# One decoder layer on one core: the modulation matvec in wider steps, wider gate columns, and a shorter last sum

## The chip, the cores and the metric

The program runs on one core of a Trainium2 chip. The metric is the device time of one execution in microseconds (us), inputs and weights in device memory, all arithmetic in f32. Engines are named as in the profile: PE (TensorE), DVE (VectorE), ACT (ScalarE), POOL (GpSimd), SP (SyncE, which here only issues DMAs).

## What is computed

One layer of a hybrid decoder, on 1024 prompt tokens and 8 single-token samples (1032 columns), model width 2048. Cut to what matters here:

```python
mod = silu(c) @ w_ada + b_ada                  # 2048 -> 3 x 2048, for 9 rows of c
shift, scale, gate = split(mod, 3)
h = rmsnorm(x, norm_g) * (1 + scale) + shift
z = h @ w_in                                   # 2048 -> 8208
y_a = b_a * conv3(c_a * h_a) * silu(g_a)       # group A, 1024 channels
o   = gated_delta_rule(conv4+silu of q|k|v, beta, decay)   # group B, 8 heads of 128, chunked
y = concat(y_a, rmsnorm(o) * silu(g_b)) @ w_out
x = x + gate * y;  return rmsnorm(x, final_g)  # and the conv and delta-rule states
```

## The kernel before

Everything is kept feature by token: a "feature tile" is 128 features on the partitions, 16 of them make up the 2048. The tokens go through in two halves of 512, the samples with the second. Each f32 product of a projection is three matmuls on rounded parts (`hh` x `whi`, `hl` x `whi`, `hh` x `wlo`); `raw` is a weight tile as loaded, `whi` and `wlo` its two parts, made by ACT and by POOL or DVE. A small planner (`_Order`) runs while the program is written. It has cost numbers for each instruction and transfer, and where code says `fill`, `pump`, `yield` or `spawn` it decides what is written next; on the chip each engine then runs its list in that order. So changed cost numbers (`_transfer`, the `cost=` of matmuls) change the order everywhere behind them.

Three places matter.

**First stage** (0 to about 169 us). The 16 tiles of x are loaded (`x`), squared and summed (`norm`, `rstd_of`). Then `w_ada` comes in 64 loads of 512 KB (`units`, `load_ada`, tiles `wat`, nine buffers), the first 2 x 2048 of its columns: shift (`s_` 0) and scale (`s_` 1). PE multiplies them with `sc` (silu of c, 9 of 32 columns used): the stationary operand has only 32 columns, so four matmuls of different k sit side by side on four strips of 32 columns of the array (`tile_position=(0, 32 * j)`), and their sums land in four bands of 32 partitions of one PSUM tile. ACT copies that to `ev`, and matmuls with the constant `selada` (10 columns) add the four bands and turn features to the partitions. DVE adds the biases into `sh` and `s1`, and `make_h` builds `hh` and `hl`. Step by step over the feature tiles (`steps`: 1, 1, then six steps of 2, then 1, 1) the tile's products with seven column groups of `w_in` are accumulated (`first_products`, PSUM tiles `pss`); `fill` puts such products between the matvec's matmuls where it expects PE to wait for a load. The stage ends with the logits' matmuls (`wlt`).

**Gates** (240 to 520 us). The third 2048 columns of `w_ada` are needed only by the output. `gate_chunks` takes them beside the first half's work: 64 loads `gw` of 256 KB (four k tiles by 128 columns), a block of 8 matmuls of 128 columns for each two of them, every `GATES` us, again on four strips; per 512 columns a copy `evg` and four `selada` matmuls.

**End.** The second half's last output product goes to `res`. `settle` squares it (ACT) and adds the square to `acc` (DVE). `final` waits for all 16, `rstd_of` sums `acc` over features with a matmul by ones, POOL takes the power, PE spreads the result, ACT copies it to `rf`. DVE (11 tiles, from PSUM) and POOL (5 tiles, from `rf`) scale the 16 tiles of `res`, and SP writes them out in 8 DMAs of two tiles.

Of the kernel before, what the change touches and what calls it, by code (L numbers as in the profile page):

```python
# [40 lines left out]
for _n, _w in [("ident", 128), ("selada", 10), ("sell", 16), ("tri", 128), ("m4", 4), ("eye", 128), ("hmask", 8),  # L41
               ("krow", 1), ("shup", 128), ("shdn", 128), ("perm", 128)]:
    CK[_n] = (_off, _w)
    _off += _w
# [5 lines left out]
def _consts():  # L50
# [4 lines left out]
    for r in range(P):  # L55
# [9 lines left out]
        if r % 32 < 9:  # L65
            c["selada"][r, r % 32] = 1
# [230 lines left out]
def _transfer(src, dst):  # L297

    n = _size(dst) * dst.shape[0]
    if src.tensor.name == "in_w_in" and int(src.offset) % 8208 // P % 8 in SLOW:  # L300
        return n * 4 / 66e3
    run = n
    for ap in (src, dst):
        r = 1
        for s, k in reversed([(int(s), int(k)) for s, k in ap.ap]):
            if s != r:
                break
            r *= k
        run = min(run, r)
    return n * 4 / (210e3 if run <= 128 else 290e3) if run >= 128 else n / run * 0.005  # L310
# [74 lines left out]
def _trunk(ctx, tc, nc, xT, w_in, w_ada, w_out, pack, consts, vecs, csq, ssm, yT, cap, cqp, ssp, cas, cqs, sss):  # L385
# [76 lines left out]
    def rstd_of(acc, n, out, now=False):  # L462
# [5 lines left out]
        yield [acc[:, :n], 2 * MARGIN]  # L468
# [3 lines left out]
        for c in range(nf):  # L472
            mm(ps[:, c:c + 1], acc[:, c * P:(c + 1) * P], ones[:, 0:1], start=True, stop=True)
        if w:
            mm(ps[:w, nf:nf + 1], acc[:, nf * P:n], ones[:, 0:1], start=True, stop=True)
            V.tensor_scalar(sm[:w, nf:nf + 1], ps[:w, nf:nf + 1], 1.0 / D, EPS, ALU.mult, ALU.add)
        V.tensor_scalar(sm[:, :nf], ps[:, :nf], 1.0 / D, EPS, ALU.mult, ALU.add)
# [7 lines left out]
        if w:  # L485
            p3 = p2[:, nf * P:n] if n <= 512 else ch_tile()[:, :w]
            mm(p3, sm[:w, nf:nf + 1].to_broadcast([w, P]), ident[:w, :w], is_transpose=True)
        S.activation(out[:, :nf * P], p2[:, :nf * P], AF.Copy)
        if w:
            S.activation(out[:, nf * P:n], p3, AF.Copy)  # L490
        if now:
            return p2
# [15 lines left out]
    def settle(t, a, b, first, fg=None):  # L508
# [12 lines left out]
        if not first:  # L521
# [862 lines left out]
    def norm():  # L1384

        ps = ch_tile()
        for k in range(NK):
# [5 lines left out]
            if k in PSQ:  # L1393
                mm(ps[:], ident, sqt[:, :HT], start=(k == PSQ[0]), stop=(k == PSQ[-1]))
                continue
            V.tensor_tensor(acc[:, :HT], acc[:, :HT], sqt[:, :HT], ALU.add)
            if k == NK - 3:
                V.tensor_tensor(acc[:, :HT], acc[:, :HT], ps[:], ALU.add)
        normed.append((yield from rstd_of(acc, HT, rstd, True)))
    PSQ, normed = (2, 5, 8, 11), []  # L1400

    hs = []
    with ExitStack() as pools:
# [18 lines left out]
        def first_products(step):  # L1422

            f, nf = steps[step]
# [30 lines left out]
        pump()  # L1455
        for step, (f, nf) in enumerate(steps):
            ps = tp_tile()
            while done < len(units) and units[done][0] == f:
                _, _, s_, k0, nk = units[done]
                wt = wats[done]  # L1460
                if k0 == 0 and s_ == 0:
                    fill(od.ready(ps[:], True))
                fill(od.ready(wt[:], False), 3)
                for k in range(k0, k0 + nk):
                    j = k % 4
                    mm(ps[32 * j:32 * j + 32, s_ * nf * P:(s_ + 1) * nf * P], sc[:, k, :],
                       wt[:, (k - k0) * nf * P:(k - k0 + 1) * nf * P], cost=0.0725 * nf,
                       start=(k < 4), stop=(k >= 12), tile_position=(0, 32 * j))
                wats[done] = None
                done += 1  # L1470
                load_ada()
                k = done - 16
                if 0 <= k < 48 and k % 3 == 0:
                    k //= 3
                    if k == 0:
                        lr_ = fx_tile("lr")
                        lr = lr_[:, :256].rearrange("p (k n) -> p k n", n=16)
                    SY.dma_start(lr[:, k, :], w_in[k * P:(k + 1) * P, 8192:8208])
                if done < len(units) and units[done][0] == f:
                    pump()  # L1480
            if step == 0:
                while not normed:
                    od.advance()
                ws.ahead(1)
            ts = []
            for k in range(f, f + nf):
                ts.append(scaled(xs0[k], HT, rstd if step else normed[0]))
                xs0[k] = None
            ev = tp.tile([P, WH], F32, tag="zr", name="ev")
            S.activation(ev[:, :2 * nf * P], ps[:, :2 * nf * P], AF.Copy)  # L1490
            pump()
            fill(od.ready(ev[:], False))
            for i in range(2 * nf):
                mm(ps[:, i * 10:i * 10 + 10], ev[:, i * P:(i + 1) * P], ck("selada"), start=True, stop=True)
            for i in range(nf):
                k = f + i
                o = (nf + i) * 10
                V.tensor_scalar(sh[:, k, :], ps[:, i * 10:i * 10 + 9], pkv("bada", k, 1), None, ALU.add)
                V.tensor_scalar(s1[:, k, :], ps[:, o:o + 9], b1[:, k:k + 1], pkv("ng", k, 1), ALU.add, ALU.mult)
            od.first(ps_g, "tp", ps)  # L1500
            if step == 0:
                pss = [mm_tile(), mm_tile(), mm_tile(), tp_tile(), ch_tile(), o_tile(), ch_tile()]
            if f % 4 == 0:
                hs += h_quad()
            for k, t in zip(range(f, f + nf), ts):
                make_h(k, t, HT, *hs[k])
            queue.append((f + nf - 1, first_products(step)))
# [22 lines left out]
    GATES = 7.0  # L1530

    def gate_chunks():
# [3 lines left out]
        def load(i):  # L1536
            f, kq = divmod(i, 4)
            wt = fx_tile("gw")
            src = w_ada[kq * 512:(kq + 1) * 512, 2 * D + f * P:2 * D + (f + 1) * P]
            SY.dma_start(wt[:, :512].rearrange("p (k n) -> p k n", n=P), src.rearrange("(k p) n -> p k n", p=P))  # L1540
            tiles.append(wt)
        for i in range(4):
            load(i)
        for f in range(NK):
            if f % 4 == 0:
                ps = mm_tile()
                od.pin(ps)
            for i in (4 * f, 4 * f + 2):
                yield GATES
                yield [tiles[i][:], tiles[i + 1][:], LAND]  # L1550
                for k in range(i % 4 * 4, i % 4 * 4 + 8):
                    j = k % 4
                    mm(ps[32 * j:32 * j + 32, f % 4 * P:(f % 4 + 1) * P], sc[:, k, :],
                       tiles[f * 4 + k // 4][:, j * P:(j + 1) * P], cost=0.096 if k % 8 else 0.18,
                       start=(k < 4), stop=(k >= 12), tile_position=(0, 32 * j))
                tiles[i] = tiles[i + 1] = None
                for j in (4, 5):
                    if i + j < 4 * NK:
                        load(i + j)
            if f % 4 < 3:  # L1560
                continue
# [302 lines left out]
```

## Time and profile before

| what | us |
|---|---|
| median of three runs (lowest, highest) | 2184.36 (2179.47, 2185.21) |
| the profiled execution: its time | 2179.28 |
| its span, first to last instruction | 2177.5 |
| PE busy in the span | 2116.6 (97%) |
| DVE, ACT, POOL busy | 1243.7, 829.3, 826.4 |

A row of the stretches view gives start and end of a stretch, its length, then busy time (and instructions) of PE, PE's weight loads, DVE, ACT and POOL, the granted PE clock (1 is full), the mean busy share of the 16 DMA engines, and GB/s. A row of the timeline gives start, duration, engine, line, operation, output<-inputs, shapes and count; in brackets stands how long the engine had been idle before it, and what released it. Each f32 matmul that is neither rounded nor a transpose appears as two records, so `x8` of the matvec is four matmuls. PE's instructions overlap, so start-to-start times say what one costs. L323 and L372 are lines of helpers that issue every instruction; a group is known by its tile names.

### The profile page before, as it was taken

What the parts mean: (1) busy time and instruction counts of PE and PEld (TensorE: products, weight loads), DVE (VectorE), ACT (ScalarE), POOL (GpSimd) and SP (SyncE); (2) the same over time, 40 slices, a digit from 0 to 9 for tenths busy, and PEclk for the clock granted to TensorE, in tenths of its full rate; (3) what the DMA queues carried; (4) which work ended last, traced back from release to release, by engine and by line L of the source; (5) the groups of instructions that cost most, each with busy time, mean ns of one, the idle gap of its engine ahead of it and who ended that gap; (6) DMA issues with size and microseconds to landing.
All of it is one profiled execution on the core that took longest, in us unless ns stands there. A gap on an engine that the chain in (4) does not pass through costs nothing. (4 is left out here: it accounts for less than half of the span.)

```text
span 2177.5 us, 40451 instructions
## 1 busy us (share of the span) xinstructions
PE 2116.6 (97%) x15045; PEld 1858.7 (85%) x15045; DVE 1243.7 (57%) x3653; ACT 829.3 (38%) x1887; POOL 826.4 (38%) x801
## 2 busy tenths in 40 slices
PE   6999999999999999999999999999999999999996
PEld 3568777777778888878889999999999999999996
DVE  3436766745967636278124747657486486345544
ACT  3224333333443432353233334343343433344553
POOL 1223333433433434332434333344433343444453
PEclk8999999999999999999999999999999999999999
DMA  9984766887544456865434565557673445878777
GB/s 298 327 237 82 157 141 152 136 134 128 135 110 92 90 99 86 76 176 177 148 108 110 122 122 106 118 101 107 105 96 82 96 100 96 90 91 231 213 215 214
DMA packets 507557, 299.65 MB, mean 138 GB/s; under 512 B 37600, under 2 KB 486880, under 8 KB 507360
## 3 DMA queue, kind: packets, MB, share of 16 engines
q1 hardware_dynamic: 484656, 285.31, 61.9%
q10 hardware_dynamic: 22704, 11.77, 2.2%
q8 instruction: 118, 1.93, 0.4%
q14 instruction: 79, 0.65, 0.1%
HBM read 277.06 MB, written 19.94 MB: 136 GB/s over the span
## 5 line engine op out<-in xcount | busy, mean ns | idle before, releaser
L323 POOL TENSOR_TENSOR wlo<-raw,whi 128x512 fp32r<-128x512 f32 x529 | 709.1, 1343 | 1242.3 <-ACT whi L323 1067.9
L372 PE MATMUL mm<-hh,whi 128*128 128x264 f32 (+1 forms) x3008 | 972.5, 323 | 6.3 <-DVE y L323 2.1
L372 PE MATMUL mm<-hl,whi 128*128 128x264 f32 (+1 forms) x3008 | 971.0, 323 | 1.9 <-DVE hl L323 1.9
L372 PE MATMUL mm<-hh,wlo 128*128 128x264 f32 (+1 forms) x3008 | 971.3, 323 | 0.3 <-POOL wlo L323 0.3
L323 ACT ACTIVATE whi<-raw 128x512 fp32r<-128x512 f32 x672 | 418.8, 628 | 622.7 <-PE mm L372 377.6
L372 PEld LDWEIGHTS mm<-hh,whi 128*128 128x128 f32 x3008 | 568.5, 189 | 54.4 <-issue 8.5
L372 PEld LDWEIGHTS mm<-hl,whi 128*128 128x128 f32 x3008 | 568.8, 189 | 43.5 <-DVE hl L323 3.6
L372 PEld LDWEIGHTS mm<-hh,wlo 128*128 128x128 f32 x3008 | 568.6, 189 | 40.4 <-issue 1.0
L372 PE MATMUL mm<-yhi,wlo 128*128 128x512 f32 (+2 forms) x768 | 248.0, 323 | 6.7 <-DVE wlo L323 4.8
L372 PE MATMUL mm<-yhi,whi 128*128 128x512 f32 (+2 forms) x768 | 246.4, 321 | 0.3 <-ACT whi L323 0.2
L372 PE MATMUL mm<-ylo,whi 128*128 128x512 f32 (+2 forms) x768 | 246.2, 321 | 0.0
L323 DVE TENSOR_TENSOR ob<-tb,xb 128x62 f32<-128x62 f32 (+30 forms) x992 | 195.7, 237 | 3.9 <-DMA tb<-ub 3.9
L323 DVE TENSOR_TENSOR xb<-xb,ob 128x62 f32<-128x62 f32 (+30 forms) x992 | 193.6, 235 | 0.0
L323 DVE TENSOR_TENSOR wlo<-raw,whi 128x512 fp32r<-128x512 f32 x143 | 107.1, 754 | 98.5 <-ACT whi L323 76.4
L372 PEld LDWEIGHTS mm<-yhi,wlo 128*128 128x128 f32 x768 | 144.5, 188 | 21.7 <-DVE wlo L323 6.9
L372 PEld LDWEIGHTS mm<-ylo,whi 128*128 128x128 f32 x768 | 144.7, 188 | 12.6 <-issue 1.0
L372 PEld LDWEIGHTS mm<-yhi,whi 128*128 128x128 f32 x768 | 144.6, 188 | 12.1 <-ACT whi L323 0.9
L323 DVE SCALAR_TENSOR_TENSOR kq<-zr,pk,kq 128x512 f32<-128x512 f32 x96 | 103.5, 1078 | 3.4
L323 DVE SCALAR_TENSOR_TENSOR res<-mm,ga,xr 128x512 f32<-128x512 f32 (+2 forms) x48 | 27.3, 569 | 110.7 <-PE mm L372 101.1
L323 DVE TENSOR_TENSOR acc<-acc,sqt 128x512 f32<-128x512 f32 (+3 forms) x71 | 54.7, 773 | 26.1 <-ACT sqt L323 25.1
L323 DVE SCALAR_TENSOR_TENSOR rt<-cht,gt_neg,v 128x128 f32<-128x128 f32 x56 | 19.5, 348 | 72.0 <-PE cht L372 72.0
L323 ACT ACTIVATE u<-cht,sm 128x128 f32<-128x128 f32 x64 | 23.5, 367 | 89.1 <-DVE u L323 76.0
(403 smaller groups left out, 1979.8 us busy)
## 6 DMA issues: line engine op xcount, KB each, us to landing
raw<-in_w_in SPq DMA_DIRECT2D x488, 256.0 KB, 5.0
raw<-in_w_out SPq DMA_DIRECT2D x160, 256.0 KB, 3.4
wat<-in_w_ada SPq DMA_DIRECT2D x64, 512.0 KB, 7.3
gw<-in_w_ada SPq DMA_DIRECT2D x64, 256.0 KB, 6.2
tb<-ub ACTq DMA_DIRECT2D x16, 512.0 KB, 6.5
raw<-in_w_in SPq DMA_DIRECT2D x48, 128.0 KB, 6.0
sl<-in_ssm SPq DMA_DIRECT2D x12, 512.0 KB, 6.3
x1s<-in_xT SPq DMA_DIRECT2D x16, 260.0 KB, 5.2
```

The costliest lines, as they stand in the source:

```text
L323: r = f(*args, **kw)
L372: r = self.pe.matmul(out, lhsT, rhs, **kw)
```

## The change

The first stage keeps its data flow, but goes in five steps of 2, 2, 4, 4 and 4 feature tiles. A `wat` load holds 4 k by 256 columns in the first two steps (rows of 1 KB in memory) and 2 k by 512 columns in the others (rows of 2 KB; before 512 B or 1 KB). A step of four takes shift and scale apart, each a full PSUM tile of 512 columns. PE takes two loads per block. The `selada` matmuls become transposes by `ident`, and DVE adds the four bands with a `tensor_reduce`. Of the sum of squares, the tiles 6, 9, 12 and 15 go through PE instead of 2, 5, 8 and 11.

The gates' loads become one k by 512 columns (2 KB rows), in 16 blocks of four matmuls of 512 columns, one per strip, every 14 us instead of every 7; the `selada` matmuls there become transposes, a reduce and one addition.

At the end the last square is kept out of `acc`: a second pair of matmuls by ones sums it, and DVE adds the two sums. The first of the scaled tiles is put ahead of ACT's copy to `rf`, and every second output DMA is issued by ACT. Some planner numbers change too.

```diff
-    return n * 4 / (210e3 if run <= 128 else 290e3) if run >= 128 else n / run * 0.005
+    return n * 4 / (210e3 if run <= 128 else 290e3 if run < 512 else 340e3) if run >= 128 else n / run * 0.005
...
-    def rstd_of(acc, n, out, now=False):
+    def rstd_of(acc, n, out, now=False, more=None):
...
-        yield [acc[:, :n], 2 * MARGIN]
+        yield [acc[:, :n], 2 * MARGIN if now else LAND]
...
+        if more is not None:
+            V.tensor_scalar(sm[:, :nf], ps[:, :nf], 1.0 / D, EPS, ALU.mult, ALU.add)
+            while not more:
+                yield 0.1
+            yield [more[0]]
+            ps = ch_tile()
+            for c in range(nf):
+                mm(ps[:, c:c + 1], more[0][:, c * P:(c + 1) * P], ones[:, 0:1], start=True, stop=True)
+            V.scalar_tensor_tensor(sm[:, :nf], ps[:, :nf], 1.0 / D, sm[:, :nf], ALU.mult, ALU.add)
...
-        if not first:
+        if keep is not None:
+            keep.append(sqt[:, a:b])
+        elif not first:
             yield [sqt[:, a:b]]
             V.tensor_tensor(acc[:, a:b], acc[:, a:b], sqt[:, a:b], ALU.add)
...
-        steps = [(0, 1), (1, 1)] + [(f, 2) for f in range(2, NK - 2, 2)] + [(NK - 2, 1), (NK - 1, 1)]
-        units = [(f, nf, s_, kq * 4 * nk, 4 * nk) for f, nf in steps for nk in (3 - nf,) for s_ in range(2)
-                 for kq in range(4 // nk)]
+        steps = ((0, 2), (2, 2), (4, 4), (8, 4), (12, 4))
+        units = [(f, nf, s_, k, 8 // nf) for f, nf in steps for s_ in range(2) for k in range(0, NK, 8 // nf)]
...
-            while most and od.now < t and queue and od.ready(hs[queue[0][0]][1], False) <= od.now:
+            while most and od.now < t and queue and max(od.ready(hs[queue[0][0]][1], False), od.now) + 0.35 < t:
...
+        def matvec(f, nf, which, then=None):
...
+                few = units[done:done + (1 if nf == 1 else 2)]
...
+                        mm(ps[32 * j:32 * j + 32, c:c + n], sc[:, k, :], wats[done][:, (k - k0) * n:(k - k0 + 1) * n],
+                           cost=0.0575 * nf + (0.18 if k == few[0][3] else 0.0), start=(k < 4), stop=(k >= 12),
+                           tile_position=(0, 32 * j))
...
+        def spread(ps, f, nf, which):
...
+            S.activation(ev[:, :n * P], ps[:, :n * P], AF.Copy)
...
+            for i in range(n):
+                mm(ps[:, i * P:(i + 1) * P], ev[:, i * P:(i + 1) * P], ident, is_transpose=True)
...
+            V.tensor_reduce(sm[:, :n, :], mk(ps[:], 0, [[P, n], [1, 9], [32, 4]]), AX.X, ALU.add)
...
-    GATES = 7.0
+    GATES = 14.0
...
+                k, f = i % NK * P, 2 * D + i // NK * 512
+                SY.dma_start(tiles[i][:, :512], w_ada[k:k + P, f:f + 512])
...
+            yield [t[:] for t in tiles[i:i + 4]] + [LAND]
+            for j in range(4):
+                mm(ps[32 * j:32 * j + 32, :], sc[:, k + j, :], tiles[i + j][:, :512], cost=0.23 if j else 0.41,
+                   start=(k == 0), stop=(k == 12), tile_position=(0, 32 * j))
...
-                    while settled.get((a, b), 0) < NK:
+                    while settled.get((a, b), 0) < NK - bi:
...
-                            V.tensor_tensor(t, t, r_[:, :b - a], ALU.mult)
+                            V.tensor_tensor(t, t, (r_ if bi else rf)[:, :b - a], ALU.mult)
+                        if bi and m == 0:
+                            S.activation(rf[:, :b - a], r_[:, :b - a], AF.Copy)
...
-                            SY.dma_start(dst, res[m // 4][:, m % 4 + 1 - n:m % 4 + 1, a:b])
+                            (S if bi and m % 4 == 1 else SY).dma_start(dst, res[m // 4][:, m % 4 + 1 - n:m % 4 + 1, a:b])
```

How the order moves is seen on PE at the start: the list up to the first product of the projection (`mm<-hh,whi`), before. `tpt<-wat,sc` are the matvec's matmuls, 16 of 128 columns being two loads; `cht<-ones,acc` and `cht<-cs,rsm` belong to the norm.

```order
L372 MATMUL cht<-sqt,cs 128x512 x4
L372 MATMUL tpt<-wat,sc 32x128 x16
L372 MATMUL cht<-ones,acc 128x1 x4
L372 MATMUL cht<-cs,rsm 128x128 x4
L372 MATMUL tpt<-cs,ev 128x10 x2
L372 MATMUL tpt<-wat,sc 32x128 x8
L372 MATMUL mm<-hh,whi 128x512
```

(A second row of 16 matvec matmuls, left out here, stands between the two rows of the norm.) Five loads are thus taken before the first product. The same list now:

```order
L370 MATMUL cht<-sqt,cs 128x512 x4
L370 MATMUL tpt<-wat,sc 32x256 x8
L370 MATMUL cht<-ones,acc 128x1 x4
L370 MATMUL tpt<-wat,sc 32x256 x16
L370 MATMUL cht<-cs,rsm 128x128 x4
L370 MATMUL tpt<-wat,sc 32x256 x8
L370 MATMUL tpt<-cs,ev 128x128 x4
L370 MATMUL tpt<-wat,sc 32x256 x16
L370 MATMUL mm<-hh,whi 128x512
```

Eight loads now stand ahead of the first transposes, and four more (the last row of 16) ahead of the first product: twelve in all.

The second place is the end of the program on DVE (its last instructions), before; `rsm` is the mean square, `res` the output tiles:

```order
L323 TENSOR_TENSOR res<-res,xr 128x8
L323 TENSOR_TENSOR acc<-acc,sqt 128x256
L323 TENSOR_SCALAR rsm<-cht 128x2
L323 TENSOR_TENSOR res<-res,cht 128x256 x11
L1849 UNCONDITIONAL_BRANCH
```

And now, with what each row waits for:

```order
L321 TENSOR_TENSOR res<-res,xr 128x8 [waits DVE_49]
L321 TENSOR_SCALAR rsm<-cht 128x2 [waits PE_49]
L321 SCALAR_TENSOR_TENSOR rsm<-cht,rsm 128x2 [waits DVE_49,PE_49]
L321 TENSOR_TENSOR res<-res,cht 128x256 [waits PE_49]
L321 TENSOR_TENSOR res<-res,cht 128x256 [waits Activation_49]
```

The addition to `acc` is gone from the end of the list and a second small operation on `rsm` is in. The first scaled tile no longer waits for ACT, but the second does, and ACT's copy in turn (not shown) waits for the first.

The third place is PE's list in the gates: the last block of a column group, with the `evg` matmuls behind it and instructions of the projection and of a head's chain between; before:

```order
L372 MATMUL mm<-gw,sc 32x128 x8
L372 MATMUL mm<-hh,whi 128x512
L372 MATMUL cht<-rt,Y 128x128
L372 MATMUL mm<-hl,whi 128x512
L372 MATMUL mm<-hh,wlo 128x512
L372 MATMUL cht<-cs,evg 128x10 x4
```

There are 32 such `gw` rows in the list, one for each two loads. Now:

```order
L370 MATMUL mm<-gw,sc 32x512 x4
L370 MATMUL mm<-hh,whi 128x512
L370 MATMUL cht<-v,Y 128x128
L370 MATMUL mm<-hl,whi 128x512
L370 MATMUL mm<-hh,wlo 128x512
L370 MATMUL cht<-cs,evg 128x128 x4
```

There are 16 such rows now, one for each four loads; the `evg` rows stay four in number.

More of the change, by code (lines that the diff above doesn't have):

```diff
@@ new lines, in _trunk, with first_norm @@
+        few0 = len([u for u in units if u[0] == 0])
+        def first_norm(done):
+            while len(normed) < (4 if done > few0 // 2 else 2):
+                od.advance()
+        lr = None
+        for step, (f, nf) in enumerate(steps):
+            if nf == 4:
+                for _ in spread(matvec(f, nf, (0,)), f, nf, (0,)):
+                    pass
+            which = (1,) if nf == 4 else (0, 1)
+            ps = matvec(f, nf, which, None if step else first_norm)
+            spreading = spread(ps, f, nf, which)
+            next(spreading)
+            ts = [scaled(xs0[k], HT, rstd if step else normed[3]) for k in range(f, f + min(nf, 2))]
@@ L1481, in _trunk @@
             if step == 0:
-                while not normed:
-                    od.advance()
+                S.activation(rstd[:, :HT], normed[3][:], AF.Copy)
                 ws.ahead(1)
[L1485 to L1491, printed above, removed]
@@ L1500, in _trunk @@
-            od.first(ps_g, "tp", ps)
+            for _ in spreading:
+                pass
             if step == 0:
                 pss = [mm_tile(), mm_tile(), mm_tile(), tp_tile(), ch_tile(), o_tile(), ch_tile()]
[L1503 to L1507, printed above, removed]
+            for k in range(f, f + nf):
+                if k % 4 == 0:
+                    hs += h_quad()
+                make_h(k, ts[k - f] if k - f < 2 else scaled(xs0[k], HT, rstd), HT, *hs[k])
+                xs0[k] = None
+                if nf == 1 or k % 2:
+                    w = min(nf, 2)
+                    queue.append((k, first_products(k + 1 - w, w)))
```

159 lines of the change are left out of this document (82 added, 77 removed).

## The prediction

> **What bounds the kernel now.** I read the page first (PE 97% busy), then the stretches view cut at the first product, the end of the first stage and the ends of the gates, then the timelines of PE and of the end.
>
> ```profile
> 32.40:56.50 24.10, 19.26 (x166) 11.63 (x164) 5.78 (x12) 2.20 (x4) 1.01 (x1) 0.92 1.09 328
> 56.50:169.30 112.80, 110.07 (x797) 70.04 (x798) 41.16 (x70) 30.84 (x50) 30.25 (x27) 0.99 0.92 269
> 169.30:240.00 70.70, 70.70 (x331) 57.88 (x330) 47.35 (x83) 35.59 (x87) 24.78 (x28) 1.00 0.50 103
> 240.00:520.00 280.00, 278.14 (x1840) 216.25 (x1839) 184.68 (x679) 98.08 (x239) 105.32 (x103) 0.99 0.79 144
> 520.00:2163.80 1643.80, 1622.54 (x11812) 1494.09 (x11810) 946.70 (x2771) 645.76 (x1480) 655.62 (x624) 1.00 0.60 123
> 2163.80:2177.50 13.70, 1.04 (x6) 0.71 (x6) 4.94 (x16) 1.31 (x3) 4.15 (x6) 0.69 0.46 153
> ```
>
> Until 56 us PE waits and the DMA engines are full (share 1.09). From 56.5 to 2163.8 PE waits 2.7 + 0 + 1.9 + 21.3 us in all, so what is taken off PE's list there comes off the end almost whole. In the last 13.7 us PE has nothing left and a chain over ACT, DVE, POOL and DMA decides.
>
> **The loads.** The rate depends on the length of a row in memory. The four stretches hold, in turn, only `x` loads (2 KB rows), `wat` loads of 128 columns (512 B), of 256 columns (1 KB), and output DMAs (1 KB):
>
> ```profile
> 6.00:14.00 8.00, 4.84 (x6) 1.30 (x6) 4.33 (x7) 7.18 (x13) 0.00 (x0) 1.00 1.05 402
> 18.00:22.00 4.00, 2.90 (x36) 2.06 (x36) 0.96 (x2) 0.00 (x0) 0.00 (x0) 0.57 1.16 290
> 50.00:59.00 9.00, 5.48 (x57) 2.55 (x56) 2.77 (x7) 3.50 (x6) 0.79 (x1) 0.84 1.10 352
> 2170.00:2175.00 5.00, 0.00 (x0) 0.00 (x0) 1.65 (x5) 0.00 (x0) 1.42 (x3) 0.50 1.04 343
> ```
>
> 524,288 B take 1.81 us at 290 GB/s, 1.49 at 352, 1.30 at 402. PE's waits for loads confirm the first two (20.19 - 18.47, 53.05 - 51.54):
>
> ```profile
> 18.47 1.08 PE L372 MATMUL tpt<-wat,sc 128*32 128x128 f32 x16 [2.81 <-DMA wat<-in_w_ada]
> 20.19 1.08 PE L372 MATMUL tpt<-wat,sc 128*32 128x128 f32 x16 [0.63 <-DMA wat<-in_w_ada]
> ...
> 31.41 1.08 PE L372 MATMUL tpt<-wat,sc 128*32 128x128 f32 x16 [2.93 <-DMA wat<-in_w_ada]
> 32.42 0.80 PE L372 MATMUL mm<-hh,whi 128*128 128x512 f32 x1
> ...
> 51.54 0.64 PE L372 MATMUL tpt<-wat,sc 128*32 128x256 f32 x8 [0.92 <-DMA wat<-in_w_ada]
> 53.05 0.64 PE L372 MATMUL tpt<-wat,sc 128*32 128x256 f32 x8 [0.87 <-DMA wat<-in_w_ada]
> ```
>
> No row shows `w_ada` in 2 KB rows; between 352 (no better than 1 KB) and 402 I take 402, since `x` goes the same way, from memory to the chip on the same queue. The Trainium skill, "DMA: Bandwidth & Descriptors", section "Where 436 GB/s comes from", speaks against it: "For HBM↔SBUF transfers the HBM side (~358) binds". By that a load would take an estimated 1.46 us, and the sum below would be some 2.6 us worse; the 402 of this trace, 8 us long, is already above it.
>
> **First stage, start.** Now twelve loads come before the first product, not five. The fifth landed at 31.41; the first four are 0.3 us shorter each (1.81 to 1.49), so it lands at 30.2, and the twelfth 7 x 1.50 later, at 40.7. With its block the first product starts at 41.5, 9.1 us later than 32.42.
>
> **First stage, PE's work.** A product costs 0.23 (46.56 to 46.79). A block of matvec matmuls between products, one load and two loads:
>
> ```profile
> 45.33 0.40 PE L372 MATMUL mm<-hh,wlo 128*128 128x512 f32 x1
> 45.65 0.64 PE L372 MATMUL tpt<-wat,sc 128*32 128x256 f32 x8
> 46.22 0.50 PE L372 MATMUL mm<-hh,whi 128*128 128x512 f32 x1
> 46.56 0.40 PE L372 MATMUL mm<-hl,whi 128*128 128x512 f32 x1
> 46.79 0.40 PE L372 MATMUL mm<-hh,wlo 128*128 128x512 f32 x1
> ...
> 88.52 1.07 PE L372 MATMUL tpt<-wat,sc 128*32 128x256 f32 x16
> 89.52 0.50 PE L372 MATMUL cht<-hh,whi 128*128 128x512 f32 x1
> 89.86 0.39 PE L372 MATMUL cht<-hl,whi 128*128 128x512 f32 x1
> ...
> 169.28 0.40 PE L372 MATMUL mm<-hh,wlt 128*128 128x512 f32 x1
> ```
>
> From start to start, less what products take anyway: 0.32 + 0.57 + 0.34 - 2 x 0.23 = 0.77 for one load, 0.43 more for two (1.00 instead of 0.57). So a block is 0.34, whatever is in it, and 0.43 per load. Counted in the lists, 59 loads in 43 blocks stand behind the first product before: 14.6 + 25.4 = 40.0 us. Now 52 loads stand there in 23 blocks: 7.8 + 22.4 = 30.2. No row shows a 512-column matmul on strips. Its block holds twice the columns of the first one above, so I take 0.34 + 0.86 = 1.20 for four; not under 0.77, the same four at half the columns, and not over four one after another, 4 x 1.13 = 4.5, by a full one alone:
>
> ```profile
> 14.53 1.13 PE L372 MATMUL cht<-sqt,cs 128*128 128x512 f32 x2 [0.85 <-ACT sqt L323]
> ...
> 69.33 0.96 PE L372 MATMUL tpt<-cs,ev 128*128 128x10 f32 x8
> 70.14 0.48 PE L372 MATMUL cht<-hh,whi 128*128 128x512 f32 x1
> ...
> 209.99 0.60 PE L372 MATMUL tpt<-cs,kq 128*128 128x128 f32 x4
> 210.35 0.47 PE L372 MATMUL mm<-hh,whi 128*128 128x512 f32 x1
> ```
>
> Four `selada` matmuls take 0.81 and four transposes 0.36, each with 0.08 around them: 0.89 and 0.44. Before, 30 matmuls in such groups (6.7 us), now seven groups of transposes (3.1).
>
> The 336 products are 77.3 us on both sides. Before: 77.3 + 40.0 + 6.7 = 124.0 of the 136.9 from 32.42 to the logits at 169.28; 12.9 were waits (4.8 + 2.7 by the first two stretches) and half clock. Now: 41.5 + 77.3 + 30.2 + 3.1 = 152.1, and then:
> - Half clock: PE has little to do before 41.5, so I let the first 12 products take twice their time: 2.4.
> - Loads: the sixteenth lands at 46.7, then sixteen of 1.30 and eleven weight tiles (1.5 MB, 5.4 us at 290) end at 73.3. PE's list up to there, from the first product, is 78 products (18), eight blocks with the loads not yet taken (11) and two groups of transposes (0.9), 32 us with the 2.4 of half clock: 73.5. Both arrive together, so each is at times late: I put 3.3. Behind that, 32 loads and their weights (some 50 us) meet 85 us of PE work, and PE bounds.
> - One PSUM tile serves all matvecs, so each next one waits for the `tensor_reduce` of the last. No row shows a reduce; on DVE it lies between 0.16 and 0.69 (next rows), nearer the first with its 144 elements, some 0.25, mostly under the 3 to 6 products that stand between (0.7 to 1.4): 0.3 six times, 1.8. Uncovered it would be 0.5 more each time.
>
> That and 0.6 of rounding make 8.1: logits at 160.2, 9.1 us earlier. With no waits it would be 14, with as many as before 4; the range for this term is 2 to 14.
>
> ```profile
> 16.78 0.69 DVE L323 TENSOR_TENSOR acc<-acc,cht 128x512 f32<-128x512 f32 x1
> 2166.04 0.16 DVE L323 TENSOR_SCALAR rsm<-cht 128x2 f32<-128x2 f32 x1 [0.70 <-PE cht L372]
> ```
>
> **Gates.** A block of eight matmuls of 128 columns has the price of one load above:
>
> ```profile
> 265.62 0.65 PE L372 MATMUL mm<-gw,sc 128*32 128x128 f32 x16
> 266.20 0.50 PE L372 MATMUL mm<-hh,whi 128*128 128x512 f32 x1
> ```
>
> 32 x 0.77 = 24.6 against 16 x 1.20 = 19.2: 5.4, and 4 x 0.45 = 1.8 by the transposes, 7.2 in all on an engine that waits 1.9 in 280 us. Chains on DVE and ACT don't get faster, so I count 6.5 (4 to 7.5). SP now waits at four `gw` loads in a row for PE's block, with weight loads queued behind; these are needed after that block too, and the DMA share there is 0.79, so nothing is charged.
>
> **End.**
>
> ```profile
> 2164.47 0.42 ACT L323 ACTIVATE sqt<-res 128x256 f32<-128x256 f32 x1 [4.17 <-DVE res L323]
> 2164.92 0.42 DVE L323 TENSOR_TENSOR acc<-acc,sqt 128x256 f32<-128x256 f32 x1 [0.48 <-ACT sqt L323]
> 2165.40 0.61 PE L372 MATMUL cht<-ones,acc 128*128 128x1 f32 x4 [1.62 <-DVE acc L323]
> 2167.50 0.38 ACT L323 ACTIVATE rf<-cht 128x256 f32<-128x256 f32 x1 [2.07 <-PE cht L372]
> 2167.92 3.73 DVE L323 TENSOR_TENSOR res<-res,cht 128x256 f32<-128x256 f32 x11 [1.71 <-ACT rf L323]
> 2168.70 4.93 SPq L323 DMA_DIRECT2D out_yT<-res  x8
> ```
>
> PE's sum starts when ACT's square ends, at 2164.9: 0.5 saved, less 0.1 for a slower small operation. The first scaled tile starts 0.4 earlier, but ACT's copy now waits for it and the second tile for the copy, so the first pair is ready 0.1 later and POOL starts 0.4 later. Two queues: the 2.1 MB of output run at 343 GB/s with the engines' share at 1.04, so a second issuer gains nothing (at most 0.9, were it the 402 of 2 KB rows; at worst the 0.4 of POOL). Net -0.3.
>
> **Sum.** -9.1 - 6.5 - 0.3 = -15.9. What a new order does to the 21.3 us of waits behind the gates can't be read before: 4 us either way, 0 taken. By the profiled execution that is 2179.3 - 15.9 = 2163.4; the median of the runs stands 5.1 higher, 2168.5 by it. I forecast the middle, **2166**. The four executions shown spread by 0.3% (2179.3 to 2185.2), which is also what I take for no change.
>
> **Rivals.**
> - Loads of 2 KB rows run no faster than 352. For: no row of `w_ada` in 2 KB, and the page's 358. Against: 402 for `x`. Sixteen loads x 0.19 = 3 us more in the first step of four, hidden later: 2169. Chance 0.10.
> - PE starves in the steps of four, waits as long as before (12.9) or its clock is halved again, as in the stretch at 50 to 59 (0.84). For: 16 loads must land before such a step's first product. Against: a whole step of products lies queued from the second one on. The stage's gain falls to 2 to 4: 2172 to 2175. Chance 0.08.
> - The new order costs what was saved: the 21.3 us of waits grow by 10 to 15: 2176 to 2182, no change. Chance 0.06.
> - Slower: matmuls of 512 columns don't overlap on the strips as those of 128 and 256 do. There are 40 such blocks (24 and 16); pairwise each costs 0.86 more, 34 us in all: 2200. It decides from 0.4 us a block on. Against: eight of 128 and four of 256 columns cost the same 0.57, so only columns count. Chance 0.04.
>
> **The numbers.** The forecast has 0.72, with 2160 to 2172 as its own range. With the ends of all terms (-22 to -8) the range is 2157 to 2176. Faster by over 0.3% (under 2177.8): 0.72 + 0.10 + 0.07 = 0.89; within: 0.07; slower: 0.04.
>
> **What would show it.** Logits near 160; first product near 41.5; loads 1.30 us apart; blocks of `gw` and 512-column `wat` at 1.2 us; 16 `gw` blocks; output DMAs still at some 340 GB/s. Waits over 30 us behind the gates, or blocks over 1.6 us, would make it wrong.

## The result and the profile after

The changed kernel takes 2313.25 us in the median (2305.92 to 2316.31) against 2182.29 (2179.47 to 2185.21): a ratio of 1.0595 (95% interval 1.0564 to 1.0626). 2166 was forecast. The profiled execution took 2316.31 us, its span is 2314.5.

The stretches view of the changed kernel, cut at the same events as before (first product, 56.5 us, logits, two times of the gates, last product, end):

```profile
41.60:56.50 14.90, 11.75 (x76) 7.67 (x72) 3.83 (x5) 2.82 (x5) 2.57 (x2) 1.00 1.07 342
56.50:165.40 108.90, 105.81 (x517) 61.84 (x518) 44.04 (x85) 29.94 (x47) 27.27 (x24) 0.98 0.88 267
165.40:240.00 74.60, 72.76 (x339) 59.29 (x338) 49.13 (x90) 35.88 (x88) 25.84 (x28) 1.00 0.60 98
240.00:520.00 280.00, 263.96 (x1378) 194.07 (x1377) 172.70 (x639) 92.66 (x227) 97.33 (x98) 0.98 0.90 135
520.00:2300.50 1780.50, 1689.76 (x11869) 1536.95 (x11868) 948.88 (x2788) 649.03 (x1492) 666.77 (x639) 0.97 0.70 115
2300.50:2314.50 14.00, 1.41 (x11) 0.99 (x9) 4.68 (x16) 1.31 (x3) 4.16 (x6) 0.63 0.46 151
```

The logits come at 165.4, 3.9 us earlier than before. The loss lies behind them, up to the last product, for the most part where the diff touches nothing. There PE waited 0 + 1.9 + 21.3 = 23.2 us; now 1.8 + 16.0 + 90.7 = 108.6. The granted clock fell from 1.00 to 0.97: by the clock's record it stood at half for 13.7 us between the logits and the last product before, now for 129.7. Half of the difference, 58 us, is an estimate of what that costs. 85.4 of waits and 58 of clock, less 3.9 in the first stage and some 7 in the gates (the prediction's term), are some 132 of the 137.0 us by which the span grew.

What PE waited for is seen in the groups (busy time, mean ns, then idle time ahead of them and its releaser) and in the DMA issues (count, KB, us from issue to landing); first of the kernel before, then of the changed one:

```profile
L372 PE MATMUL mm<-hh,whi 128*128 128x264 f32 (+1 forms) x3008 | 972.5, 323 | 6.3 <-DVE y L323 2.1
L323 ACT ACTIVATE whi<-raw 128x512 fp32r<-128x512 f32 x672 | 418.8, 628 | 622.7 <-PE mm L372 377.6
raw<-in_w_in SPq DMA_DIRECT2D x488, 256.0 KB, 5.0
```

```profile
L370 PE MATMUL mm<-hh,whi 128*128 128x264 f32 (+1 forms) x3008 | 982.1, 326 | 33.3 <-ACT whi L321 17.5
L321 ACT ACTIVATE whi<-raw 128x512 fp32r<-128x512 f32 x672 | 418.5, 628 | 769.0 <-DMA raw<-in_w_in 312.1
raw<-in_w_in SPq DMA_DIRECT2D x488, 256.0 KB, 7.0
```

Before, ACT waited with its `whi` copies for PE to release a buffer; now it waits for `raw`, and PE for ACT. These 488 loads are the same in both kernels, 512 rows of 512 B each, and they take 7.0 us where they took 5.0. They differ by where in `w_in` they read. The view of the tile `raw` for successive loads of the column tiles 31 and 7 (128 columns each; both are number 7 modulo 8), before and after:

```profile
L323 SPq DMA_DIRECT2D raw<-in_w_in x7: 367/368/368, 899.8 to 918.3; - x7
DMA to landing us min/median/max: 10.8/12.6/13.3
```

```profile
L321 SPq DMA_DIRECT2D raw<-in_w_in x8: 367/368/1117, 962.3 to 990.8; - x8
DMA to landing us min/median/max: 10.0/19.4/20.7
```

The table below is worked out from the traces and the order in which each program issues its loads: loads of `w_in` that were queued behind another one of it (issued some 0.9 us or more before that one landed), the mean time from the landing of that one to their own, by the number of the column tile modulo 8. An entry rests on some 13 to 55 loads, in the last two rows on 5 to 17. Eight tiles are 4,096 B, and a row of `w_in` is 32,832 B, 8 x 4,096 + 64.

```
tile mod 8            0    1    2    3    4    5    6    7    us
before               4.0  2.4  1.7  2.2  1.8  1.9  2.3  3.7
after                3.0  2.9  2.0  2.9  2.2  2.5  2.6  5.6
after, 64 ahead      2.5  2.6  2.3  2.3  2.3  2.2  2.9  4.7
after, 960 ahead     4.5  2.8  2.5  1.9  2.4  1.7  2.1  3.0
after, 976 ahead     4.0  2.6  1.9  2.0  2.1  1.8  2.2  3.7
before, 64 ahead     3.2  3.5  2.2  2.8  2.0  2.7  2.8  5.6
gates alone          2.9  2.9  2.1  2.4  2.1  2.3  2.6  4.8
before, long rows    1.6  1.3  1.0  1.7  1.6  1.4  1.5  1.4
after, long rows     1.7  1.3  0.9  1.5  1.5  1.3  1.5  1.4
```

PE uses a weight tile up in 12 products of 0.23 us, 2.8 us. A tile that takes longer than that starves PE, unless others are ahead in store. Before, 0 and 7 took longer, and the planner knows it: a line of `_transfer`, with `SLOW = (0, 7)`, counts those columns at 66 GB/s. Now 0, 1 and 3 lie at the limit and 7 takes twice as long as PE can wait.

### The profile page after: what moved, and what is told of

It reads as the page before. It is cut to its first block, busy times and chain, and to the rows that moved or that the text cites. A ratio compares the mean times of both kernels' runs of the same rounds, so it can differ in the third digit from the quotient of the medians.

```text
span 2314.5 us, 38944 instructions
## 1 busy us (share of the span) xinstructions
PE 2165.6 (94%) x14297; PEld 1867.5 (81%) x14297; DVE 1236.9 (53%) x3647; ACT 827.1 (36%) x1885; POOL 827.3 (36%) x807
## 5 line engine op out<-in xcount | busy, mean ns | idle before, releaser
L370 PE MATMUL mm<-hh,wlo 128*128 128x264 f32 (+1 forms) x3008 | 982.2, 327 | 10.3 <-POOL wlo L321 9.3
L370 PEld LDWEIGHTS mm<-hh,whi 128*128 128x128 f32 x3008 | 576.2, 192 | 91.2 <-ACT whi L321 23.4
L370 PEld LDWEIGHTS mm<-hh,wlo 128*128 128x128 f32 x3008 | 576.2, 192 | 63.3 <-POOL wlo L321 18.0
L370 PEld LDWEIGHTS mm<-hl,whi 128*128 128x128 f32 x3008 | 576.4, 192 | 45.0 <-issue 3.4
L321 DVE TENSOR_TENSOR xb<-xb,ob 128x62 f32<-128x62 f32 (+30 forms) x992 | 184.4, 226 | 0.0
L370 PEld LDWEIGHTS mm<-yhi,whi 128*128 128x128 f32 x768 | 146.6, 191 | 12.6 <-ACT whi L321 1.3
L321 DVE TENSOR_SCALAR u<-cht,sm 128x128 f32<-128x128 f32 x64 | 22.3, 348 | 71.3 <-PE cht L370 71.3
```

The source lines that it names most:

```text
L321: r = f(*args, **kw)
L370: r = self.pe.matmul(out, lhsT, rhs, **kw)
```

## The experiments

**What moved the loads?** The diff drops `selada` from the constants: they are 5,120 B shorter in device memory, and every tile behind them on the chip moved by 32 B. Four runs set this apart from the new order. First, the columns back in both places:

```diff
-for _n, _w in [("ident", 128), ("sell", 16), ("tri", 128), ("m4", 4), ("eye", 128), ("hmask", 8),
+for _n, _w in [("ident", 128), ("selada", 10), ("sell", 16), ("tri", 128), ("m4", 4), ("eye", 128), ("hmask", 8),
```

> The changed kernel with the ten columns of selada put back into the constants, unused: the constants are 807 columns again in device memory and on the chip, every address as in the kernel before; the order of the instructions stays that of the changed kernel. Theory P (place in device memory: the weights w_in lie at other addresses because the constants got 5,120 B shorter, and their loads by 512 B rows run slower): the loads of w_in take 5.0 us again in the median (7.0 in the changed kernel), PE's waits behind 169 us fall to some 25 us, 2150 to 2185 us. Theory S (place on the chip: every tile moved by 32 B): the same. Theory O (the new order alone brings the waits): no change, 2305 to 2320 us with loads of 7.0.

2310.65 us, ratio 1.0597 (1.057 to 1.0623). Then in device memory alone and on the chip alone:

```diff
-    return np.concatenate([c[n] for n in CK], axis=1)
+    return np.concatenate([c[n] for n in CK] + [np.zeros((P, 10), np.float32)], axis=1)
```

> The changed kernel with ten columns of zeros behind the constants in device memory alone; on the chip all tiles stay where the changed kernel has them. P: as the first run of this call, 2150 to 2185 us, loads of w_in 5.0 us. S and O: 2305 to 2320, loads of 7.0.

```diff
-    cs = cp.tile([P, LATE], F32, name="cs")
+    cs = cp.tile([P, LATE + 10], F32, name="cs")
```

> The changed kernel with the tile of the constants ten columns wider on the chip, so that all tiles behind it lie as before; device memory stays as in the changed kernel. S: 2150 to 2185 us. P and O: 2305 to 2320.

2305.38 and 2303.33 us (one execution each, as in the next three runs). And the kernel before with the shorter constants:

```diff
-    return np.concatenate([c[n] for n in CK], axis=1)
+    return np.concatenate([c[n] for n in CK if n != "selada"], axis=1)
...
+    nc.vector.tensor_reduce(cs[:, P:EARLY], mk(cs[:], 0, [[1, 10], [32, 4]]), AX.X, ALU.add)
```

> The kernel before, in its own order, but with the constants 797 columns wide in device memory: selada is not loaded, DVE makes it from the identity with one reduce at the start. On the chip all addresses stay. P: the loads of w_in take some 7 us as in the changed kernel, and the kernel before becomes slower by most of what the changed one lost, 2250 to 2320 us. S and O: no change, 2179 to 2188, loads of 5.0.

2184.88 us. The issue row of `raw` in the first of the four, then in the fourth:

```profile
raw<-in_w_in SPq DMA_DIRECT2D x488, 256.0 KB, 6.8
```

```profile
raw<-in_w_in SPq DMA_DIRECT2D x488, 256.0 KB, 4.9
```

P in its narrow form and S fall: neither the constants' size nor the place on the chip does it. That left the order (O), or the place of `w_in` moved by something else. So the array itself was moved, the order left alone:

```diff
-("w_in", f["w_in"][0])
+("w_in", np.concatenate([np.zeros(SHIFT, np.float32), f["w_in"][0].reshape(-1)]))
+    args[1] = bass.AP(args[1].tensor, SHIFT, [[8208, 2048], [1, 8208]])
```

> The changed kernel, same order, with w_in moved within its array: 960 zeros (3,840 B) stand ahead of it in device memory. Ground: in the kernel before, the loads of w_in whose column tile is 0 or 7 (mod 8, so by their place in 4 KB) follow each other 4.0 and 3.7 us apart when queued, the others 1.7 to 2.4; in the changed kernel tile 7 takes 5.6, tile 0 3.0, the others 2.0 to 2.9. Theory A (the slow places are fixed in device memory, and the array starts some 256 B further on in the changed program, whatever its constants): 3,840 B more, 4,096 in all, give the pattern of before, 0 and 7 at 3.7 to 4.0 and the others near 2; 2155 to 2190 us. Theory O (the order of the program alone): 2295 to 2320 us, pattern as in the changed kernel.

> The same with 64 zeros (256 B) ahead of w_in. A: the slow place moves by half a column tile further, to 6 and 7 at some 3.5 to 4 each and 7 no longer at 5.6; the time is 2170 to 2290 us, since the planner counts 0 and 7 as slow. O: 2295 to 2320, tile 7 at 5.6.

2206.74 and 2220.29 us: 107 and 93 us less by moving an array and nothing else. With 960 zeros the slow place lies on 0 and 7 again, though at 4.5 and 3.0 and with a time 17 us above what A had put. With 64 tile 7 still holds most of it (4.7) and 6 little (2.9), a smaller move than A's 3.5 to 4 for both; the time is within A's range.

> The kernel before, in its own order, with 64 zeros (256 B) ahead of w_in. A: the slow place moves from 0 and 7 to 7 alone, at 5 to 6 us as in the changed kernel; 2230 to 2320 us. O: 2176 to 2195 us.

4143 us: PE's matmuls of the projection took 523 ns in this one execution instead of 323, without a cause that the trace shows, so its time says nothing. The same once more:

> The kernel before with 64 zeros (256 B) ahead of w_in, again: in its one run before this, PE ran all its matmuls at half their rate (523 ns instead of 323) without any record of the clock, so that its time (4143 us) says nothing of the place. Tile 7 did take 5.8 us there. Theory A (the place of w_in decides how fast its column tiles load): tile 7 at 5 to 6 us, PE's waits behind the logits 60 us or more instead of 26, 2230 to 2320 us. Theory O (the order decides): 2176 to 2195.

2322.05 us, ratio 1.0663 (1.0633 to 1.0694): the kernel before, in its own order, loses all that the changed one lost, by 256 B. Its table row is near that of the changed kernel (tile 7 at 5.6 in both, tile 1 at 3.5 against 2.9). And the changed kernel, set back finely:

> The changed kernel with 976 zeros (3,904 B) ahead of w_in. With 960, tile 0 took 4.5 and tile 7 3.0 us; in the kernel before they take 4.0 and 3.7. A: 64 B less far back brings both to 3.5 to 4.2, and the time to 2165 to 2205 us (2206.7 with 960). O: 2295 to 2320.

2182.96 us, ratio 1.0016 (1.0005 to 1.0027), with nearly the table row of before. The issue row of `raw` in the moved kernel before, and in this one:

```profile
raw<-in_w_in SPq DMA_DIRECT2D x488, 256.0 KB, 6.6
```

```profile
raw<-in_w_in SPq DMA_DIRECT2D x488, 256.0 KB, 5.1
```

A is shown in what it says of the cause: moving `w_in` in device memory, with the order left alone, takes 130 us off the changed kernel and puts 142 on the one before. That the array starts elsewhere in the changed program, by some 192 to 256 B going by the shifts that undo and that make the loss, is inferred from the table: no start address was read. What lets it start there stays open. The function `gate_chunks` of the changed kernel with its `GATES`, alone in the kernel before, changes the pattern too:

> The kernel before with the gates of the changed one alone (16 blocks of four matmuls of 512 columns, loads of 2 KB rows, every 14 us); first stage, end and constants stay. By the prediction's term: 6.5 us less, 2172 to 2180. Theory A says no more than whether the array's place moves with this program too (then the pattern shows it, and 2250 or more). Theory O with the gates as its cause: 2230 to 2320 us, waits behind 240 us; with the first stage as its cause: 2172 to 2182.

2233.31 us in one execution, tile 7 at 4.8, so that this run says nothing of what the gates cost. By its time theory O with the gates as cause (2230 to 2320) would do as well, and A's 2250 is missed. But the new pattern is there up to 230 us, ahead of the first gate load (tile 1 at 2.8 against 2.3 in the kernel before), and behind 520 us, when the last has landed (tiles 0 and 7 at 2.9 and 4.7 against 4.0 and 3.7), so the gates' own traffic doesn't make it.

**Away with the slow place.** Rows of 33,280 B instead of 32,832:

```diff
-("w_in", f["w_in"][0])
+("w_in", np.pad(f["w_in"][0], ((0, 0), (0, 8320 - 8208))))
```

> The kernel before with rows of w_in 8320 floats long in device memory (33,280 B, 65 x 512) instead of 8208 (32,832 B, that is 8 x 4,096 + 64); zeros behind each row, loads of the same size and number, same order. A, if the 64 B step per row makes the slow tiles: no column tile is slower than another, all 1.5 to 2.5 us queued; PE's waits fall by 5 to 15 us, 2160 to 2180 us. O: 2176 to 2186. If the rows' length only moves the slow place, tiles of another number take 4 to 6 us and the time is 2190 to 2320.

> The changed kernel with the same longer rows. A: even tiles as in the run before this one, the waits behind the logits 26 us or less; the change is then worth what its own terms are: 5 to 16 us less than the kernel before with these rows, 2145 to 2175 us. O: 2295 to 2320.

2166.25 us (ratio 0.9949, 0.9935 to 0.9962) and 2171.09 (0.9968, 0.9957 to 0.9979). No tile is slow any more, and those that never were slow load faster too (0.9 to 1.7 us, where A had put 1.5 to 2.5). 33,280 B are 65 x 512, so that with the long rows a load's 512 B pieces start at the same place within 512 B in every row, and with 32,832 they don't; whether that or the 64 B step within 4 KB counts, these runs don't tell apart. The issue row of `raw` reads the same in both:

```profile
raw<-in_w_in SPq DMA_DIRECT2D x488, 256.0 KB, 2.9
```

The Trainium skill, "DMA: Bandwidth & Descriptors", section "Latency and other measured facts", tells of such an effect at row pitches of 2 and 4 MiB: copies from device memory to device memory at some three quarters and at half the rate, the latter restored by 4 KiB more per row and not by 192 B. The effect agrees in kind; but these runs have it at a pitch of 32,832 B, 448 B more remove it, and the place of the first byte decides as well.

With even loads the change is still worth nothing: 4.8 us more than the kernel before with the same rows, where 5 to 16 less was expected. Product by product, the changed kernel is 6.9 us ahead at the logits (160.7 against 167.6) and 16.0 ahead at 578 us; at 652 us it is 2.2 behind. The place in between, in the stretches view of the kernel before, then of the changed one, both with long rows:

```profile
606.00:660.00 54.00, 52.74 (x260) 43.10 (x259) 39.69 (x124) 23.39 (x62) 18.36 (x24) 0.97 0.37 107
```

```profile
606.00:635.00 29.00, 19.07 (x79) 14.87 (x78) 22.20 (x132) 8.61 (x27) 4.16 (x7) 0.59 0.14 42
```

And the timeline of PE there in the changed one with long rows:

```profile
605.95 0.39 PE L371 MATMUL mm<-hh,wlo 128*128 128x512 f32 x1
606.26 0.67 PE L371 MATMUL cht<-X,dU 64*64 64x64 f32 x8
...
611.97 0.80 PE L371 MATMUL cht<-u,kt 128*128 128x128 f32 x2 [2.94 <-DVE u L322]
...
617.14 1.87 PE L371 MATMUL cht<-ones,acc 128*128 128x1 f32 x8 [0.86 <-DVE acc L322]
620.55 0.20 PE L371 MATMUL cht<-ones,acc 128*8 128x1 f32 x2 [1.54 <-DVE rsm L322]
...
630.84 0.76 PE L371 MATMUL cht<-u,kt 128*128 128x128 f32 x2 [0.84 <-DVE ob L322]
631.39 0.64 PE L371 MATMUL ot<-u,dA 128*128 128x128 f32 x2
631.68 0.77 PE L371 MATMUL mm<-hh,whi 128*128 128x512 f32 x1
```

From 606.0 to 631.7 PE's list has no product at all, only a head's chain, link by link with its waits for DVE, and the sum of squares of the second half. PE waits 9.9 us, and the clock drops to 0.59. This is written so: in `head`, the loop `while recd[half] < len(queue) - 2: od.advance()` writes no further product until, by the planner's reckoning, the chain of two heads back is done (read from the code; no run changes the loop itself). Is that order the fault of the planner's numbers, or are the chains the bound? With the long rows no tile is slow, so the planner was told so:

```diff
-SLOW = (0, 7)
+SLOW = ()
```

> The changed kernel with rows of w_in 8320 floats long, and the planner told that no column tile is slow (SLOW empty), which is so with these rows (1.3 to 1.7 us each). With the longer rows alone the changed kernel took 2171.1 and the kernel before 2166.3. Up to 578 us it was 16.0 us ahead of that one; between 606 and 632 us its PE did nothing but a head's chain and the statistics of the second half, with waits, and the clock at half for 23.9 us. Theory T1 (the order is to blame: the planner counts the tiles 0 and 7 as slow and stops the projection there): the stretch goes, with a half clock of 7 us at most; 2148 to 2159 us. Theory T2 (the heads' chains on DVE bound this stage, so that whatever PE saves ahead is given back at the next wait for them): 2163 to 2174, with as much wait elsewhere before 720 us.

> The kernel before with the longer rows and SLOW empty. T1: its order had little of such a stretch (half clock 3.4 us there), so 2160 to 2168 us, and the changed kernel of this call is 5 to 16 us below it. T2: 2160 to 2168 too, and the changed kernel no more than 3 below it.

2157.51 us (ratio 0.9902, 0.9885 to 0.9918) and 2163.41 (0.9926, 0.9911 to 0.9941). 13.6 us come back to the changed kernel by numbers alone, as T1 said. Not all of T1 came: 10.2 us of half clock stayed at 590 us, where it put 7 at most. Now the two parts of the change by themselves, with long rows and SLOW as it was: `gate_chunks` of the changed kernel in the kernel before, and that of before (with `selada`) in the changed one:

> The kernel before with the new gates alone, rows of 8320 floats, SLOW as it was. By the prediction's term 6.5 us below the 2166.3 of the kernel before with these rows: 2158 to 2162. If the gates bring the stretch in which the projection stands still: 2164 to 2178, with waits and half clock between 550 and 640 us.

> The changed kernel with the old gates, rows of 8320 floats, SLOW as it was: first stage and end are new. By the prediction's terms 9.4 us below 2166.3; by the logits of the changed kernel with these rows (160.7 against 167.6) 7: 2156 to 2161. If the first stage brings the stretch: 2164 to 2178, with waits and half clock between 550 and 640 us.

2164.99 us (0.9932, 0.9913 to 0.9951) and 2170.5 (0.9957, 0.9941 to 0.9974). Both miss their terms in the same manner: 1.3 us less and 4.3 more than 2166.25. Against the kernel before with long rows, product by product, the gates alone are 9.1 us ahead at 546 us and 0.4 behind at 595, with waits of 2.91 and 2.50 us and 6.8 of half clock in between; the first stage alone is 7.1 ahead at 601 and 1.0 behind at 650, with a wait of 3.29 and 10.2 of half clock. Whichever part brings the lead, it is gone behind this place.

In the run with SLOW empty the logits came at 166.8, not 160.7. The sixteen small loads `lr` start at column 8192, tile 64, which counts as 0 mod 8: by the empty list their cost number grew fivefold, and the first stage's order with it. The last pair undoes that:

```diff
-    if src.tensor.name == "in_w_in" and int(src.offset) % ROW // P % 8 in SLOW:
+    if src.tensor.name == "in_w_in" and int(src.offset) % ROW // P == 64:
```

> As the changed kernel with longer rows and SLOW empty (2157.5 us), but the 16 small loads lr of the logits' weights keep the cost number that they had while column tile 64 counted as slow. With SLOW empty the planner gave them five times that number, and the first stage's order changed with it: logits at 166.8 us, with the old numbers 160.7. The order now agrees with the old one up to some 380 us and has the new one's later part in kind. If the two parts add: logits at 160 to 161, 2149 to 2155 us. If what the first stage gains is given back at the heads' chains again (theory T2 of the call before): 2156 to 2160.

```diff
-                            (S if bi and m % 4 == 1 else SY).dma_start(dst, res[m // 4][:, m % 4 + 1 - n:m % 4 + 1, a:b])
+                            SY.dma_start(dst, res[m // 4][:, m % 4 + 1 - n:m % 4 + 1, a:b])
```

> The same with all output DMAs of the end issued by SP, none by ACT. In the changed kernel the first of the eight is issued 4.73 us after the last product and the last lands at 13.11; in the kernel before, on SP alone, it is 5.06 and 12.86 (both with longer rows). If two queues cost time by landing unevenly (1.8 us between the sixth and the seventh): SP alone lands the last at 12.4 to 12.7, 0.4 to 0.7 us less in all. If the DMA engines bound it either way: 12.9 to 13.2, the same time within 0.2.

2151.04 us (ratio 0.9864, 0.9846 to 0.9881) and 2150.72 (0.9865, 0.985 to 0.9881). The parts add, and T2 falls: logits at 162.1 (160 to 161 was expected), 12.0 us ahead of the kernel before with long rows at 970 us, 13.8 at the last product. In the stretches view of the first of the two the place in question is whole:

```profile
578.00:640.00 62.00, 60.91 (x334) 48.64 (x334) 45.22 (x173) 23.09 (x60) 19.33 (x23) 0.97 0.32 85
```

This version beats both kernels, the one before by 29 us; 15 of them are left against the kernel before with long rows (2166.25), and 12 against that one with SLOW empty (2163.41). So with even loads, and a list that holds work for PE, the change is worth 12 to 15 us, not far from the 15.9 of the sum. It asks for an input array with padded rows. With SP alone the last output lands 13.15 us after the last product, with two queues 12.64 in this pair and 13.11 in the changed kernel with long rows: no difference that could be told from chance.

## Why the prediction was wrong

**The step that failed** is the one on the waits behind the gates: "4 us either way, 0 taken". It took for granted that loads which the diff leaves alone keep their time. They did not: 7.0 us for 5.0, 85 us of waits, 58 of clock. No term, no rival and no bound held that, the slower rival (matmuls on strips that don't overlap) named the wrong cause, and the range ended 137 us short. The sign named for being wrong, waits over 30 us behind the gates, came: 90.7. What could have been read blind: in the trace of before the loads of tile 7 took 12.6 us (the row above) with the others near 5, and the planner's `SLOW` named two tiles; where a load's time hangs on its address, a bound of 4 us needed the array to keep its place. That the place would move could not be read from either.

**At an equal place** the sum would still have failed. With the place set back the ratio is 1.0016, where the terms said 0.993. There too PE's list has no product between 609.4 and 635.1 us, and the clock stands at half for 23.9 us: the stop at the heads' loop, which no term held. By terms:

- First stage, -9.1. In the changed kernel -3.9, with the place set back -5.2 (169.3 to 164.1), with long rows -6.9 (167.6 to 160.7): all inside the range of 2 to 14. The first product came where it was put (41.5), but in part by luck: with the place set back it comes at 39.3, because the eight `raw` loads ahead of it take 4.0 us there and 6.6 in the changed kernel. The timeline of PE in the changed kernel at the first product, and at a block of four 512-column matmuls, then a row of its stretches view:

```profile
41.61 0.50 PE L370 MATMUL mm<-hh,whi 128*128 128x512 f32 x1
...
64.22 1.07 PE L370 MATMUL tpt<-wat,sc 128*32 128x512 f32 x8
65.22 0.50 PE L370 MATMUL mm<-hh,whi 128*128 128x512 f32 x1
65.55 0.39 PE L370 MATMUL mm<-hl,whi 128*128 128x512 f32 x1
```

```profile
66.50:71.50 5.00, 5.00 (x30) 2.34 (x28) 2.14 (x7) 0.63 (x1) 2.16 (x1) 1.00 1.06 382
```

  Such a block costs 1.20 as forecast (1.00 for the block itself, 65.22 - 64.22, and the same around it); so the rival of strips that don't overlap falls. Loads of 2 KB rows run at 382 GB/s where they fill the queues, that is 1.37 us a load: nearer the 402 taken than the 352 of the rival. The Trainium skill's 358 for this direction ("DMA: Bandwidth & Descriptors", section "Where 436 GB/s comes from") is below what this trace shows. What was mis-sized: the waits behind the first product, 3.3 us for loads and 1.8 for the reduce. With long rows they are 6.5, of which one is 5.03, with the clock at half for 6.8 (half clock was taken for the first products alone, 2.4 us, and they had none); in the changed kernel this wait is 3.8. By its name it is a wait for the reduce, but it begins with a load, as the timeline of the changed kernel with long rows shows:

```profile
53.53 0.63 ACT L322 ACTIVATE whi<-raw 128x512 fp32r<-128x512 f32 x1 [5.25 <-DMA raw<-in_w_in]
54.19 0.69 DVE L322 TENSOR_TENSOR wlo<-raw,whi 128x512 fp32r<-128x512 f32 x1 [12.25 <-ACT whi L322]
56.01 0.30 DVE L322 TENSOR_REDUCE sm<-tpt 128x36 f32<-128x144 f32 x1
56.36 5.35 PE L371 MATMUL tpt<-wat,sc 128*32 128x512 f32 x24 [5.03 <-DVE sm L322]
```

  In DVE's list the reduce stands behind a `wlo`, which waits through ACT for a `raw` load. The reduce itself takes 0.30, near the 0.25 taken.
- Gates, -6.5. The blocks cost 1.20 where they didn't have to wait, and with even loads the lead grew by 9.1 us from the logits to 578 us, more than the term (1.0 of it is fewer waits). It was given back at the heads' loop. The prediction said that a chain on DVE and ACT would take some of it; it took all, since the list there held nothing else for PE.
- End, -0.3. The tail behind the last product was 14.0 against 13.7; over the traces of this case it is 13.4 to 14.4 with this end and 13.7 to 14.5 with the one of before, so that 0.3 can't be told from chance. The steps came as told, by the timeline of the changed kernel:

```profile
2301.69 0.61 PE L370 MATMUL cht<-ones,sqt 128*128 128x1 f32 x4 [0.82 <-ACT sqt L321]
2303.80 0.42 DVE L321 TENSOR_TENSOR res<-res,cht 128x256 f32<-128x256 f32 x1 [1.30 <-PE cht L370]
2304.26 0.38 ACT L321 ACTIVATE rf<-cht 128x256 f32<-128x256 f32 x1 [2.07 <-DVE res L321]
2305.12 3.45 ACTq L321 DMA_DIRECT2D out_yT<-res  x4
```

  The first output is issued 4.6 us after the last product instead of 4.9, but the last one lands 13.0 after it instead of 12.7.

**The rivals.** "The new order costs what was saved" (chance 0.06, 10 to 15 us of new waits) is what the even rows show: 8.7 us more of waits behind the logits up to 1150 us and 20.5 more of half clock, 18 us of loss between 578 us and 970. The half clock, which the rival hadn't counted, makes about as much of it as the waits. "PE starves in the steps of four" came in part: ahead of the first such step PE waits 3.8 us in the changed kernel and the clock drops to half again, and the stage's gain of 3.9 is within that rival's 2 to 4; with long rows it is 6.9.

## What to carry to other kernels

Before a change is costed, look at the loads that bound the kernel and ask whether their time depends on where they read: group them by address, not by line. If some are several times slower, the time of the kernel hangs on the array's place, which another program may not keep; a row length that makes them even (here 448 B more per row: -13 us for the kernel before, and no slow tile in either program) comes first, and the planner's numbers must follow it. A lead won on one engine is only kept if the list holds other work for it at the next point where it meets a slower chain.

## What the runs showed of the hardware

256 B more ahead of an array, in the same program, cost 142 us of 2180. A load of 256 KB in 512 B pieces, one per row, takes 1.7 to 5.6 us when queued, by its place in 4 KB, with rows 32,832 B apart, and 0.9 to 1.7 with rows 33,280 B apart. Why the memory does so, no run shows.

Short waits are dear: with PE's waits of 0.3 to 2.9 us between 606 and 632 us (changed kernel, long rows), 9.9 in all, the clock stood at half for 23.9 us. PE was busy for 17.1 of them, so an estimate of what that cost is half of this, 8.5 us. The Trainium skill, "TensorE: Matmul & The Clock Gate", section "Part 1: The HAM clock gate", tells of a free-running activity window of 3.4 us; the pieces of half clock here are 3.4, 6.8, 10.2 and 23.9 us, multiples of it.
